# Transposing a block's attention result one tile later in the first half of the prompt

## The chip, the cores and the metric

The kernel runs on one core of one Trainium2 chip. The metric is the device time of one execution in microseconds (us). A core has five engines that run side by side and meet only through semaphores: PE multiplies matrices (PEld is its loading of weights), DVE and ACT work on vectors, POOL does small vector work and issues indirect loads, SP issues loads and stores. Each engine takes its instructions in a fixed order. PE writes into PSUM, eight banks of 128 x 512 floats; DVE and ACT read a result out of a bank, and only then can PE write that bank again.

## The reference

One layer of a decoder is computed for a prompt of 1024 rows and for 8 single sample rows. The part that the change touches is causal attention over the prompt (8 heads of 64, blocks of 128 query rows), with a bias c that is a running sum of forget gates:

```
s = jnp.einsum('bqhd,bkhd->bhqk', q, k).astype(jnp.float32) * (ATT_HEAD_DIM ** -0.5)
s = s + (cq.astype(jnp.float32).transpose(0, 2, 1)[:, :, :, None]
         - ck.astype(jnp.float32).transpose(0, 2, 1)[:, :, None, :])
s = jnp.where(kpos[None, :] <= qpos[:, None], s, -jnp.inf)
p = jax.nn.softmax(s, axis=-1).astype(v.dtype)
return jnp.einsum('bhqk,bkhd->bqhd', p, v)
```

Around it stand RMSNorms, an input projection, a spatial-gating branch, the output projection, cross-attention into 256 memory rows and a gated feed-forward part with a short convolution. The sample rows do the same, with attention over 8192 cached positions each, whose keys and values are gathered from pages in memory.

## The kernel before

The prompt is worked in two halves of 512 rows (`hf` 0 and 1). `attention(hf)` runs over 4 pairs of heads (`hp`), 2 blocks of 256 query rows (`blk`), and in each block 4 tiles of 128 x up to 512 (first half) or up to 1024 (second half) scores: 2 heads times 2 row groups. For each tile `scores` has PE write the scores into a bank `ba` (lines 807, 809, 811), DVE take the negated row maximum `mx` (813) and ACT the exponential with its row sum (814; in the second half 816 and 817).

What follows a tile is put in a list, `queue`, and taken from it later, so that PE has other tiles' scores to work on while DVE and ACT finish. `turn` transposes the exponentials with PE (836) and copies them out of PSUM (843 by ACT, in the second half also 841 by DVE). When a block's four tiles are turned, `values` multiplies them with v (852), ACT copies the product out (861), and DVE takes the reciprocal of the row sums (863). `back` transposes that product again, in two transpositions (872), and DVE writes them, scaled, into `att` (874, two instructions). After each tile `drain(LA[hf])` runs the list down to 2 entries. `fin` is the entry that runs `values` and then inserts `back` into the list at place `BKQ`, which is 1.

The banks for `turn`, `values` and `back` come from `B3`, which counts its calls: every third call gets the bank `ms`, of which there is one, the other two get one of the two banks `bb`. So it is the order of the calls that decides who gets `ms`. In the first half a block makes six calls, and so the same two places get `ms` in each block. The decode work uses `ms` too, for small products (1410, 1460, 1473).

Other work is woven in by generators: in the first half the memory's key and value projections (lines 272 to 274 with their splits 235 and 236, and 720) and then the gating branch (649, 659, 641, 678), and all through it the sample rows' attention: loads from the caches by POOL (1420 and 1482), multiplications and reductions by DVE (1427, 1428), products by PE (1488, bank `dv`). `setup` prepares the next pair of heads: transpositions of q and k (750, 779), copies (757, 784, 774, 788), POOL's copies (758, 785) and loads (759 of `cq_d`, 771 of `ck_d`).

The code fixes which operations there are and their order within a dependency, but not the final order on each engine: a scheduler goes over the traced instructions with estimated costs and lets a later instruction go ahead where it is ready sooner. A small change in the traced order is so carried on into other places.

Of the kernel before, what the change touches and what calls it, by code (L numbers as in the profile page):

```python
# [73 lines left out]
BKQ = 1  # L74
# [4 lines left out]
def build(nc, tc, ctx, a, phases=None):  # L79
# [31 lines left out]
    def U(shape, dt=F32):  # L111
        n = 1
        for s in shape[1:]:
            n *= s
        t = upool.tile([P, UW], dt, tag="u", bufs=NU, name=nm("u"))[:, :n]
        if len(shape) == 3:
            t = t.rearrange("p (a b) -> p a b", b=shape[2])
        return t

    def T2(n=512, dt=F32):  # L120
        return tpool.tile([P, 512], dt, tag="t2", bufs=NT, name=nm("t2"))[:, :n]
# [4 lines left out]
    def sm(shape, tag, bufs=2, dt=F32):  # L126
        return small.tile(shape, dt, tag=tag, bufs=bufs, name=nm(tag))
# [598 lines left out]
    def attention(hf, late=None, at=3):  # L726
# [3 lines left out]
        def load(hp):  # L730
            cs = slice(hp * P, (hp + 1) * P)
            qn = tpool.tile([P, 512], F32, tag="qn", bufs=1, name=nm("qn")).rearrange("p (i c) -> p i c", c=P)
            nc.sync.dma_start(qn, q_d[hf * 512 : (hf + 1) * 512, cs].rearrange("(i p) c -> p i c", p=P))
            if hf == 0:
                kvn = U([P, 2 * nk, P])
                kn, vn = kvn[:, :nk, :], kvn[:, nk:, :]
            else:
                kn, vn = T2().rearrange("p (i c) -> p i c", c=P), U([P, nk, P])
            nc.sync.dma_start(kn, k_d[hf * 512 : nk * P, cs].rearrange("(i p) c -> p i c", p=P))
            nc.sync.dma_start(vn, v_d[: nk * P, cs].rearrange("(i p) c -> p i c", p=P))  # L740
            return qn, kn, vn
# [53 lines left out]
        def scores(qkv, ls, blk, j, ii):  # L795

            qab, ka, kb, _ = qkv
            i = blk * 2 + ii
            e = (hf * 4 + i + 1) * P
            nch = 1 if e <= 512 else 2  # L800
            n = e // nch
            p_ = (WRAW(e) if PW else U([P, e])) if hf else T2(e)
            mx = sm([P, 1], "mx", 4)
            both = BA2().rearrange("p (c n) -> p c n", c=2)[:, :, :n] if nch == 2 else BA()[:, :n].unsqueeze(1)
            for ch in range(nch):
                s = both[:, ch, :]
                mmul(s, qab[j][:, 0, i * P : (i + 1) * P], ka[j][:, ch * n : ch * n + n], start=True, stop=False)
                diag = ch == nch - 1
                mmul(s, qab[j][0:68, 1, i * P : (i + 1) * P], kb[j][0:68, ch * n : ch * n + n], start=False, stop=not diag)
                if diag:  # L810
                    mmul(s[:, n - P :], ident_b, cmask_b, start=False, stop=True)
            if nch == 1:
                nc.vector.tensor_reduce(mx, s, axis=AX.X, op=ALU.max, negate=True)
                nc.scalar.activation(p_[:, :e], s, AF.Exp, bias=mx, accum_out=ls[:, ii, j : j + 1])
            else:
                nc.vector.tensor_reduce(mx, both, axis=AX.XY, op=ALU.max, negate=True)
                nc.scalar.activation(
                    p_[:, :e].rearrange("p (c n) -> p c n", c=2), both, AF.Exp, bias=mx, accum_out=ls[:, ii, j : j + 1]
                )
            lastexp[:] = [newest(ENG.Activation)]  # L820
            return p_
# [23 lines left out]
        def values(qkv, ls, pt, hp, blk):  # L845
            vn = qkv[3]
            nkt = hf * 4 + blk * 2 + 2
            po = B3()
            for kt in range(nkt):
                for j in range(2):  # L850
                    q0 = P if kt == nkt - 1 else 0
                    mmul(
                        po[64 * j : 64 * j + 64, q0:256],
                        vn[:, kt, 64 * j : 64 * j + 64],
                        pt[j][kt // 4][:, kt % 4, q0:256],
                        start=(kt == 0),
                        stop=(kt == nkt - 1),
                        tile_position=(0, 64 * j),
                    )
            ot = T2(256)  # L860
            nc.scalar.activation(ot, po[:, :256], AF.Copy)
            rl = sm([P, 4], "rl", 3)
            nc.vector.reciprocal(rl, ls.rearrange("p i j -> p (i j)"))
            return ot, rl, hp, blk
# [16 lines left out]
        queue = []  # L881

        def drain(n):
            while len(queue) > n:
                queue.pop(0)()
# [10 lines left out]
        for hp in range(4):  # L896
            for _ in nxt or ():
                pass
            qkv, nxt = got.pop(), None
            if hf == 0 and hp == 2:  # L900
                phase[0] = "attx"
            for blk in range(2):

                if hp == at and late and (blk == 0 or hf == 0):
                    late()
                ls = sm([P, 2, 2], "ls", 3)
                pt = []
                nkt = hf * 4 + blk * 2 + 2
                for j in range(2):
                    for ii in range(2):  # L910
                        p_ = scores(qkv, ls, blk, j, ii)
                        if ii == 0:
                            pt.append(
                                [
                                    (U([P, 4, 256]) if nkt - g > 2 else T2(512).rearrange("p (a b) -> p a b", b=256))
                                    for g in range(0, nkt, 4)
                                ]
                            )
                        queue.append(partial(turn, p_, pt[j], nkt - 1 + ii, ii))
                        if j == 1 and ii == 1:  # L920

                            def fin(*args):
                                r = values(*args)
                                queue.insert(min(BKQ, len(queue)), partial(back, *r))

                            queue.append(partial(fin, qkv, ls, pt, hp, blk))
                        drain(LA[hf])
                        yield 1.8
                        if hp < 3 and (blk, j, ii) == LD[hf]:
                            raw = load(hp + 1)  # L930
                        if hp < 3 and (blk, j, ii) == ST[hf]:
                            nxt = setup(hp + 1, *raw)
                        if nxt:
                            next(nxt, None)
                            yield 1
# [1089 lines left out]
```

## Time and profile before

| | us |
|---|---|
| median of 3 executions | 1793.09 (1792.41 to 1802.47) |
| the profiled execution | 1796.66 |
| its span in the trace | 1794.9 |
| first half's attention, about | 262 to 372 of the span |
| second half's attention, about | 372 to 493 |

The trace has a busy time for each engine. PE's is modelled, since its matmuls are pipelined: a matmul of 512 columns is shown as 0.39 us long while the next one starts 0.23 us after it. So a busy PE need not be at its best rate, but an idle PE is lost time wherever PE is what the kernel waits for. A row of the timeline has its start in the span, its length, engine, line, operation and operands, and in brackets how long the engine sat idle before it and what released it.

### The profile page before, as it was taken

To read this page: it belongs to the slowest core of one execution; us is meant where nothing else is said; L and a number is where in the kernel's file an instruction comes from. 1 tells how busy PE (TensorE), PEld (TensorE's weight loads), DVE (VectorE), ACT (ScalarE), POOL (GpSimd) and SP (SyncE) were. 2 spreads that over 40 slices of the span, in tenths; PEclk is the share of its full clock that TensorE was granted. 3 is DMA by queue.
4 is the path that set the end of the run, shared out by engine and by line. 5 is a ranking of instruction groups with operands and counts; after the bars stand their busy time and mean duration, and the time that the engine had idled before them with its cause. 6 is when DMAs were issued, how large, how long until landed. Compare 5 with 4: busy or idle time off the path is not lost.

```text
span 1794.9 us, 25099 instructions
## 1 busy us (share of the span) xinstructions
PE 1736.6 (97%) x9637; PEld 1286.9 (72%) x9637; DVE 1399.3 (78%) x1733; ACT 734.4 (41%) x1374; POOL 496.1 (28%) x461
## 2 busy tenths in 40 slices
PE   8999999889999999999999999999999999999997
PEld 5887777655677667777777777776676778767875
DVE  4689658988788987999999999887885549855344
ACT  6332256466643635333333244335353233333332
POOL 1252334432222332233322223333322122102110
PEclk9999999999999999999999999999999999999999
DMA  8886888787697975779788878978879687568982
GB/s 299 304 295 222 301 324 318 260 274 230 254 401 279 366 300 222 287 289 349 293 304 311 289 309 318 382 292 331 312 288 343 221 301 250 192 259 299 358 311 81
DMA packets 157075, 521.07 MB, mean 290 GB/s; under 512 B 20874, under 2 KB 40842, under 8 KB 124186
## 3 DMA queue, kind: packets, MB, share of 16 engines
q0 software_dynamic: 57168, 341.14, 50.2%
q1 hardware_dynamic: 92874, 165.73, 26.6%
q10 hardware_dynamic: 6912, 12.59, 1.9%
q8 instruction: 76, 1.25, 0.3%
q14 instruction: 45, 0.37, 0.1%
HBM read 495.47 MB, written 23.93 MB: 289 GB/s over the span
## 4 chain that ended last, share of the span: by engine, by line
PE 53%; DMA 9%; issue 8%; DVE 6%; POOL 2%; ACT 2%; POOLq 0%; DVEq 0%; ACTq 0%; SPq 0%
DMA kv<-cache_v,io 7%; PE ba L272 6%; PE ba L274 6%; PE ba L273 6%; PE dv L1488 4%; PE bb L272 3%; PE bb L273 3%; PE bb L274 3%; PE ba L1065 1%; PE ba L1064 1%; PE ba L1066 1%; PE dv L331 1%; DVE kv L1436 1%; PE dv L1764 1%; DVE s L1440 1%
## 5 line engine op out<-in xcount | busy, mean ns | idle before, releaser
L235 ACT ACTIVATE wh<-wr 128x1024 fp32r<-128x1024 f32 (+2 forms) x220 | 228.7, 1044 | 438.9 <-PE ba L273 152.7
L236 DVE TENSOR_TENSOR wl<-wr,wh 128x1024 fp32r<-128x1024 f32 (+2 forms) x220 | 263.0, 1200 | 165.7 <-PE ba L274 58.0
L1420 POOL DMA_INDIRECT kv<-cache_k,io x128 | 188.8, 1475 | 589.2 <-DVE s L1440 317.7
L1436 DVE TENSOR_TENSOR kv<-kv,d 128x1024 f32<-128x1024 f32 (+1 forms) x156 | 258.0, 1681 | 25.0 <-DMA kv<-cache_k,io 25.0
L1440 DVE TENSOR_REDUCE s<-kv 128x16 f32<-128x1024 f32 (+1 forms) x156 | 258.4, 1673 | 0.0
L1482 POOL DMA_INDIRECT kv<-cache_v,io x128 | 168.7, 1318 | 243.2 <-PE dv L1488 155.6
L272 PE MATMUL ba<-u,wh 128*128 128x512 f32 x528 | 209.8, 398 | 0.0
L273 PE MATMUL ba<-u,wh 128*128 128x512 f32 x528 | 208.8, 395 | 0.5 <-DVE u L239 0.5
L274 PE MATMUL ba<-u,wl 128*128 128x512 f32 x528 | 209.2, 397 | 0.0
L272 PE MATMUL ba<-wh,u 128*128 128x512 f32 (+1 forms) x495 | 186.1, 379 | 0.9 <-ACT u L235 0.9
L273 PE MATMUL ba<-wl,u 128*128 128x512 f32 (+1 forms) x495 | 185.3, 375 | 1.5 <-DVE wl L236 1.5
L274 PE MATMUL ba<-wh,u 128*128 128x512 f32 (+1 forms) x495 | 183.2, 375 | 0.0
L1488 PE MATMUL dv<-kv,s 128*32 128x512 f32 x1024 | 126.5, 600 | 4.6 <-DMA kv<-cache_v,io 4.6
L274 PEld LDWEIGHTS ba<-u,wl 128*128 128x128 f32 x528 | 99.5, 188 | 28.3 <-issue 5.7
L272 PEld LDWEIGHTS ba<-u,wh 128*128 128x128 f32 x528 | 99.6, 189 | 26.6 <-issue 4.8
L273 PEld LDWEIGHTS ba<-u,wh 128*128 128x128 f32 x528 | 99.6, 189 | 25.1 <-issue 2.3
L272 PEld LDWEIGHTS ba<-wh,u 128*128 128x128 f32 x495 | 93.0, 188 | 25.0 <-issue 6.5
L272 PE MATMUL bb<-u,wh 128*128 128x512 f32 x272 | 108.6, 399 | 0.0
L273 PE MATMUL bb<-u,wh 128*128 128x512 f32 x272 | 107.9, 397 | 0.1
L274 PE MATMUL bb<-u,wl 128*128 128x512 f32 x272 | 107.9, 397 | 0.0
L273 PEld LDWEIGHTS ba<-wl,u 128*128 128x128 f32 x495 | 93.1, 188 | 20.7 <-DVE wl L236 2.5
L274 PEld LDWEIGHTS ba<-wh,u 128*128 128x128 f32 x495 | 92.9, 188 | 19.4 <-issue 1.6
(451 smaller groups left out, 3311.9 us busy)
## 6 DMA issues: line engine op xcount, KB each, us to landing
wr<-w_up SPq DMA_DIRECT2D x88, 512.0 KB
kv<-w_up POOLq DMA_DIRECT2D x22, 1024.0 KB
wr<-w_down SPq DMA_DIRECT2D x40, 512.0 KB
kv<-w_down POOLq DMA_DIRECT2D x11, 1024.0 KB
wr<-w_in SPq DMA_DIRECT2D x16, 512.0 KB
wr<-w_o SPq DMA_DIRECT2D x16, 512.0 KB
wr<-w_cq SPq DMA_DIRECT2D x16, 512.0 KB
wr<-w_co SPq DMA_DIRECT2D x16, 512.0 KB
```

The lines of the kernel that those rows point to most:

```text
L235: nc.scalar.activation(h, src, AF.Copy)
L236: nc.vector.tensor_tensor(l, src, h.bitcast(F32), op=ALU.subtract)
L272: mmul(out, sh, mh, start=(i == 0), stop=False)
L273: mmul(out, sh, ml, start=False, stop=False)
L274: mmul(out, sl, mh, start=False, stop=(i == n - 1))
L331: mmul(ps[32 * j : 32 * j + 32, :w], xT[:, k, :] if nk == 8 else xT[:, k * 8 : k * 8 + 32], raw[:, q, j * w : (j + 1) * w], start=(k == 0) ...
L1064: mmul(pss[i], mh[k][:, tb], wh, start=(k == korder[0]), stop=False)
L1420: nc.gpsimd.indirect_dma_start(kv, None, a["cache_k"], off(kidx[:, b, ch : ch + 1]))
L1436: nc.vector.tensor_tensor(kvv[:, i : i + m, :], kvv[:, i : i + m, :], qb.unsqueeze(1).broadcast_to((P, m, 512)), op=ALU.mult)
L1440: nc.vector.tensor_reduce(s[:, ch * 4 + i : ch * 4 + i + m, :].rearrange("p k h -> p (k h)"), kvv[:, i : i + m, :].rearrange("p k (h d) -> ...
L1482: nc.gpsimd.indirect_dma_start(kv, None, a["cache_v"], off(kidx[:, b, ch : ch + 1]))
L1488: mmul(dv[32 * j : 32 * j + 32, :], s[:, ch * 4 : ch * 4 + 4, :].rearrange("p k h -> p (k h)"), kvv[:, j, :], start=(ch == 1), stop=(ch == ...
```

## The change

`back` is inserted one place further behind in the list in the first half. The second half's code keeps its place.

```
                             def fin(*args):
                                 r = values(*args)
-                                queue.insert(min(BKQ, len(queue)), partial(back, *r))
+                                queue.insert(min(BKQ if hf else BKQ + 1, len(queue)), partial(back, *r))
```

Within one block the traced order was: `values` of the block before, turn 1, `back`, turn 2, turn 3 and, with the next block's first tile, turn 4. It is now: `values`, turn 1, turn 2, `back`, turn 3, turn 4. With it the banks change: `ms` went to `values` and turn 2 before, and goes to `values` and `back` now; all four turns now have `bb`. The last block's `back` has nothing to go behind and stays where it was. The scheduler then arranges the whole anew, so rows move on all engines, from the first half's attention through the second's, and again in a stretch around 1200 to 1350 us of the span.

PE at the third pair of heads, first block (names with `t_567` are the product that is transposed back, `t_563` a tile's exponentials, `qn` the next pair's q):

```order
-L811 MATMUL ba_3190<-cmask_b,ident_b 128x128
-L872 MATMUL bb_3183<-cp,t_567_3163 128x128 x2
-L836 MATMUL ms_3196<-cp,t_563_3150 128x128 x4
+L811 MATMUL ba_3191<-cmask_b,ident_b 128x128
+L836 MATMUL bb_3183<-cp,t_563_3150 128x128 x4
+L872 MATMUL ms_3197<-cp,t_567_3163 128x128 x2
 L836 MATMUL bb_3202<-cp,t_570_3174 128x128 x3
+L750 MATMUL bb_3215<-cp,qn_3209 128x128 x4
```

The four transpositions of turn 2 now stand ahead of the two of `back`, the two have traded banks, and the second half's first transpositions of q (line 750) have come forward by two tiles of scores.

PE at the last pair of heads, first block (`ms_3361` is the product, `t_626` its copy):

```order
-L872 MATMUL bb_3384<-cp,t_626_3366 128x128 x2
-L836 MATMUL ms_3397<-cp,t_622_3353 128x128 x4
+L836 MATMUL bb_3384<-cp,t_622_3353 128x128 x4
+L852 MATMUL ms_3361<-t_594_3251,u_3040 64x256
+L852 MATMUL ms_3361<-t_606_3300,u_3040 64x256
+L852 MATMUL ms_3361<-t_594_3251,u_3040 64x128
+L852 MATMUL ms_3361<-t_606_3300,u_3040 64x128
+L872 MATMUL ms_3398<-cp,t_626_3366 128x128 x2
 L836 MATMUL bb_3403<-cp,t_629_3375 128x128 x3
+L852 MATMUL ms_3416<-u_3341,u_3040 64x256
```

Here turn 2 has moved ahead of `values` as well, so that the transpositions of `back` still stand directly behind the product that they take. The next block's product needs the same bank `ms` three transpositions later.

POOL where the second half's attention is set up (`u_3220` and `u_3230` are the two heads' q, `kv` a buffer for the decode's cached values):

```order
 L758 COPY u_3220<-u_3220 64x512
-L1482 DMA kv_3506<-cache_v,io 128x2048
 L759 DMA u_3230<-cq_d 4x512
 L771 DMA u_3235<-ck_d 4x1024
 L758 COPY u_3230<-u_3230 64x512
+L1482 DMA kv_3506<-cache_v,io 128x2048
```

An indirect load of cached values, which stood between the two heads' set-up, is now behind both.

## The prediction

> **What bounds the kernel now.** I read the page's busy times first, then a table of stretches, then who waited for whom in the stretches that the change touches, then the timeline at each of the places.
>
> ```profile
> PE 1736.6 (97%) x9637; PEld 1286.9 (72%) x9637; DVE 1399.3 (78%) x1733; ACT 734.4 (41%) x1374; POOL 496.1 (28%) x461
> ```
>
> PE is busy for 97% of 1794.9 us, so 58.3 us of idle PE is all that any reordering could take out of the whole kernel. The table of stretches says where that lies (first columns: from and to, length, then busy us and instructions of PE, PEld, DVE, ACT, POOL, then PE's granted clock):
>
> ```profile
> 262.00:310.00 48.00, 47.71 (x260) 35.23 (x259) 37.40 (x62) 30.45 (x66) 19.97 (x23) 1.00 0.82 301
> 310.00:330.00 20.00, 16.36 (x102) 11.48 (x100) 19.81 (x31) 8.38 (x18) 8.44 (x11) 1.00 1.02 347
> 310.00:372.00 62.00, 51.57 (x338) 37.79 (x337) 57.00 (x116) 35.59 (x96) 27.61 (x37) 0.98 0.84 282
> 372.00:493.00 121.00, 108.95 (x758) 73.45 (x757) 101.03 (x167) 75.33 (x154) 33.98 (x44) 0.97 0.73 243
> 493.00:1795.00 1302.00, 1275.05 (x6957) 943.10 (x6955) 1019.45 (x1204) 489.00 (x904) 335.06 (x294) 0.99 0.79 294
> ```
>
> Up to 310 us PE idles 0.3 us: with the projections' matmuls to fill in, nothing waits. From 310 to 372, where the first half's attention has little beside it, PE idles 10.4 us, but DVE is 92% busy (57.00 of 62) and idles only 5.0 us, and from 310 to 330 only 0.2 us. There a gap on PE is mostly the shadow of a full DVE, and closing it on PE alone moves the wait elsewhere. In the second half's attention PE idles 12.0 us and DVE 20.0: there it is the length of the chain scores, maximum, exponential, transposition that leaves gaps.
>
> PE's waits between 262 and 493 us, by what released them (total, times, longest):
>
> ```profile
> PE ba L807 <- ACT wr L817: 5.2, 6, 1.9
> PE ms L852 <- DVE dec L1412: 2.7, 1, 2.7
> PE bb L872 <- ACT t L861: 2.6, 4, 1.1
> PE bb L750 <- DVE u L874: 0.6, 1, 0.6
> ```
>
> The edit's own targets are the third and fourth: the transpositions of `back` wait for ACT's copy of the product, 2.6 us in four places, and one later step waits for a bank that `back` holds. So the prize named by the change is 3.2 us of 1794.9, 0.2%. One percent is 17.9 us here, about what a measurement of this kernel can tell from no change.
>
> **The change part by part.** No instruction is added or removed: the same eight pairs of transpositions and eight pairs of DVE writes, the same copies. Only places and banks move. The waits that it can reach are these, with what replaced each:
>
> ```profile
> 337.70 0.47 ACT L814 ACTIVATE t<-ba,mx 128x256 f32<-128x256 f32 x1
> 338.76 1.77 PE L852 MATMUL ms<-u,u 128*64 128x256 f32 x16 [0.37 <-DVE m L1463]
> 341.01 0.44 PE L872 MATMUL bb<-cp,t 128*128 128x128 f32 x2 [0.47 <-ACT t L861]
> 341.28 0.38 PE L836 MATMUL ms<-cp,t 128*128 128x128 f32 x2
> 352.40 0.68 ACT L814 ACTIVATE t<-ba,mx 128x512 f32<-128x512 f32 x1
> 353.50 0.44 PE L872 MATMUL bb<-cp,t 128*128 128x128 f32 x2 [1.07 <-ACT t L861]
> 356.50 0.66 PE L750 MATMUL bb<-cp,qn 128*128 128x128 f32 x4 [0.62 <-DVE u L874]
> 369.25 0.44 PE L872 MATMUL bb<-cp,t 128*128 128x128 f32 x2 [0.57 <-ACT t L861]
> 376.00 0.44 PE L872 MATMUL bb<-cp,t 128*128 128x128 f32 x2 [0.47 <-ACT t L861]
> ```
>
> At 338.76 PE sits 0.37 us before `values`, until DVE has read a decode result out of `ms`. The two transpositions of turn 2 (0.38 us at 341.28) now stand ahead of it, and their exponentials were done at 337.70 + 0.47 = 338.17, so they fill that hole: -0.4 us. The wait of 0.47 at 341.01 stays, because `back` still stands right behind its product there.
>
> At 353.50 `back` waits 1.07 us. Turn 2 goes first now, and its exponentials were done at 352.40 + 0.68 = 353.08, so PE starts 0.42 us sooner and has the copy by the time it gets to `back`: -0.4. At 356.50 the transpositions of q wait 0.62 for the bank `bb` of that same `back`; `back` is no longer in a `bb`: -0.6. At 369.25 turn 2 has moved ahead of `values`, `back` stands behind `values` as before, and 0.57 stays. The last block's `back`, at 376.00, is not moved (the fourth of the four waits).
>
> The set-up of the second half is the next piece. Along the chain that ended last and on POOL stand, with line 759 loading `cq_d` and 771 `ck_d` for the second head's q:
>
> ```profile
> 359.11 1.07 POOL L1482 DMA_INDIRECT kv<-cache_v,io  x1 [0.23 <-DVE mx L813]
> 360.15 0.58 POOL L759 DMA_DIRECT2D u<-cq_d  x1
> 360.68 5.60 DMA u<-ck_d
> 366.28 0.59 ACT u L784
> 367.33 0.55 PE L836 MATMUL bb<-cp,t 128*128 128x128 f32 x3 [1.37 <-ACT t L843]
> 388.70 1.04 PE dv L1488 x8
> ```
>
> POOL's indirect load at 359.11 now goes behind the set-up, so that the loads of 360.15 and after are issued 1.07 us earlier; the chain from there runs through the load to ACT's copy at 366.28 and to PE's wait of 1.37 at 367.33. I take -1.1 (ends: 0, if the copy waits for something else, and the whole wait, -1.4). What was ahead and is now behind, the decode's cached values, is used by PE at 388.70, 29 us later, and costs nothing as long as that lead lasts.
>
> One large wait I count at nothing:
>
> ```profile
> 316.83 0.87 PE L852 MATMUL ms<-t,u 128*64 128x256 f32 x8 [2.72 <-DVE dec L1412]
> 329.30 0.56 DVE L813 TENSOR_REDUCE mx<-ba 128x1 f32<-128x384 f32 x1
> 330.62 0.55 PE L836 MATMUL bb<-cp,t 128*128 128x128 f32 x3 [1.54 <-ACT t L814]
> ```
>
> The new order puts 24 projection matmuls ahead of that `values`, so the 2.72 us at 316.83 should go. But at 330.62 PE waits for exponentials that wait for DVE's maximum at 329.30, and DVE up to there was full (19.81 of 20) with the same instructions in either order. PE would arrive earlier and wait longer: 0, with -2.7 as the end.
>
> Against this stands the bank. `values` and `back` both have `ms` now, and the next `values` must wait until DVE has done the pair at 874. From the end of the two transpositions to the end of DVE's pair it took, at the seven places that move (here the first, the longest and the last):
>
> ```profile
> 293.41 0.39 PE L872 MATMUL bb<-cp,t 128*128 128x128 f32 x2
> 295.25 0.48 DVE L874 TENSOR_TENSOR u<-bb,rl 128x128 f32<-128x128 f32 x2
> 327.10 0.39 PE L872 MATMUL bb<-cp,t 128*128 128x128 f32 x2
> 329.78 0.48 DVE L874 TENSOR_TENSOR u<-bb,rl 128x128 f32<-128x128 f32 x2
> 370.06 0.49 DVE L874 TENSOR_TENSOR u<-bb,rl 128x128 f32<-128x128 f32 x2
> 299.57 0.39 PE L274 MATMUL bb<-wh,u 128*128 128x512 f32 x1
> 299.80 0.39 PE L272 MATMUL bb<-wh,u 128*128 128x512 f32 x1
> ```
>
> That is 1.93, 2.77 and, behind the 369.25 above, 0.86 us; all seven sum to 11.0. In the new order most have more than that between `back` and the next use of `ms`: 24 projection matmuls behind the longest, each 0.23 us after the other as the last two rows show, four tiles' scores behind the first. Only the last has just three transpositions there (0.5 us): 0.86 - 0.5, so +0.4. The ends are 0 and +11.0.
>
> Sum: -0.4 - 0.4 - 0.6 - 1.1 + 0.4 = -2.1 us. Against the profiled execution's 1796.66 that makes 1794.6; that execution lies 3.6 above the median, and from 1793.09 it makes 1791.0. The second half's attention is reordered too, without a direction that I can read; I take 0 and as its ends plus or minus 5.2, its largest group of waits. Behind 493 us PE is busy for 1275 of 1302 us, so what is won before arrives at the end.
>
> The clock adds an uncertainty of its own:
>
> ```profile
> 365.00:369.60 4.60, 2.66 (x24) 2.02 (x24) 4.54 (x8) 4.03 (x11) 1.60 (x3) 1.00 1.07 357
> 369.70:373.10 3.40, 3.40 (x16) 2.98 (x15) 0.91 (x4) 2.92 (x9) 0.00 (x0) 0.51 1.04 428
> 379.90:383.20 3.30, 3.30 (x16) 2.99 (x16) 3.30 (x7) 1.83 (x6) 1.64 (x2) 0.50 0.02 3
> 407.30:410.50 3.20, 3.20 (x17) 1.65 (x16) 3.20 (x5) 0.00 (x0) 0.43 (x1) 0.50 0.08 29
> ```
>
> After 4.6 us in which PE was 58% busy the clock stood at 0.51 for 3.4 us, which costs 3.4 x 0.49 = 1.7 us. The last two rows are two more such stretches. One more or one fewer is 1.7 us; I take none. The Trainium skill (TensorE: Matmul & The Clock Gate, section on HAM oscillation) says that the clock falls for idle gaps beyond about 3.4 us; the longest wait before this stretch was 1.37, so the trace does not agree, and by that rule the term would be 0 and the sum the same -2.1.
>
> **The rivals.** First, slower: the shared bank decides. If DVE is late at all seven places and PE stands at the next `ms` each time, the seven lags are waits: 1793.1 + 11.0 = 1804.1. For it: DVE is 92% busy there, and `ms` also serves the decode. Against it: the matmuls that stand between. It decides from the point where the work between `back` and the next `ms` is shorter than DVE's lag. The Trainium skill (Perfetto Trace Analysis, section on optimizing Tensor performance, matmuls) has the rule that speaks for this rival: independent matmul groups should rotate through different banks so that one's evacuation overlaps the next one's matmuls, and two successive groups in the one `ms` do not; the row at 356.50 shows such a wait with two banks already.
>
> Second, nothing arrives: PE comes earlier and waits for DVE, the second half's new order gives back what is left, or `back` still stands behind its product, as it does at two of seven places by the order. That gives 1793.1, and with its 5.2 up to 1798.3.
>
> Third, more is won than I count: all 5.0 us of DVE's idle time between 310 and 372, 5.2 in the second half, and all three slow-clock stretches (5.1): 15.3 us, 1777.8. For it, that PE's gaps and the clock feed each other; against it, that it needs all three.
>
> **How the numbers follow.** My forecast has 0.42, the first rival 0.25, the second 0.17, the third 0.12; 0.04 is for what I don't see. The likeliest case gives 1791.0. Its own range is 1784 to 1798 (the 5.2 and one stretch of the clock either way, 6.9). The whole range reaches to the first rival with one stretch more, 1804.1 + 1.7 = 1806; the low end stays at 1784, which leaves most of the third rival out, and the first rival's tail above: together less than 2 in 10. Slower by over 1% (above 1811.0) needs all seven lags, the second half's 5.2 and a slow stretch more; faster by over 1% (below 1775.2) needs more than the third rival has. 0.09 and 0.05, the rest, 0.86, within 1%.
>
> **What would show it.** In the changed kernel's trace: no wait at 872 above 0.6 us, no wait of line 750 for 874, line 852's wait for the decode gone while the wait of 836 for 814 behind it grows, PE's idle time from 310 to 372 between 7 and 11 us. The first rival would show as a group of PE `ms` waits on DVE's 874 of several us. I am wrong if PE's idle time between 262 and 493 us changes by more than 10 us, or if time appears in a stretch behind 493 us.

## The result: slower by half a per cent, and not where the edit is

| | changed | before, on the same chip | ratio, 95% interval |
|---|---|---|---|
| first set | 1808.18 us, 8 executions (1803.24 to 1809.86) | 1795.63, 8 executions | 1.0065 [1.0051, 1.0079] |
| second set (run e1) | 1805.13 us, 6 executions (1801.74 to 1806.09) | 1794.48, 28 executions | 1.0053 [1.0035, 1.0071] |

So the change costs 0.5 to 0.7%, about 9.5 to 11.7 us. It is within the 1% that the largest chance was given to, but the sign is wrong, and the first set lies just above the range. Its interval is 0.14% either way, so far less than the one percent of the prediction can be told from no change here. The profiled execution took 1803.24 us, the least of its eight; its span is 1801.5. The page's busy times for it:

```profile
PE 1738.0 (96%) x9637; PEld 1283.4 (71%) x9637; DVE 1398.1 (78%) x1733; ACT 730.7 (41%) x1374; POOL 490.3 (27%) x461
```

The instructions are the same, and PE is busy for 1.4 us more in a span that is 6.6 us longer. So in this execution most of the loss is idle PE, and the table of stretches tells where. Of the changed kernel:

```profile
262.00:310.00 48.00, 47.11 (x258) 34.76 (x256) 35.17 (x58) 29.81 (x66) 17.18 (x23) 1.00 0.85 304
310.00:330.00 20.00, 17.51 (x96) 12.25 (x94) 19.87 (x32) 8.82 (x18) 7.76 (x11) 0.91 0.96 331
310.00:372.00 62.00, 53.62 (x331) 37.72 (x329) 56.04 (x115) 33.22 (x87) 27.14 (x38) 0.94 0.79 269
372.00:493.00 121.00, 108.45 (x781) 73.23 (x778) 103.42 (x175) 77.14 (x164) 35.24 (x43) 1.00 0.75 256
493.00:640.00 147.00, 140.21 (x708) 102.45 (x707) 127.51 (x158) 68.82 (x153) 48.12 (x32) 1.00 0.89 337
1160.00:1345.00 185.00, 175.40 (x874) 122.58 (x872) 156.88 (x186) 82.58 (x182) 61.59 (x49) 0.98 0.85 316
493.00:1801.00 1308.00, 1275.60 (x6946) 940.25 (x6944) 1019.02 (x1202) 486.21 (x903) 337.48 (x293) 0.99 0.78 292
```

The two stretches of the kernel before that were not shown yet:

```profile
493.00:640.00 147.00, 144.69 (x735) 107.08 (x734) 130.20 (x163) 70.15 (x154) 44.84 (x34) 1.00 0.92 348
1160.00:1345.00 185.00, 175.04 (x886) 124.89 (x885) 153.94 (x185) 81.99 (x178) 59.78 (x49) 0.97 0.83 309
```

In the stretch of the edit and of the second half's attention, 262 to 493 us, PE idles 0.9 + 8.4 + 12.6 = 21.8 us, against 0.3 + 10.4 + 12.1 = 22.8 before. Behind 493 us the same 1275 us of work now take 1308 instead of 1302. Most of that, in these two executions, is between 493 and 640, where PE idles 6.8 us instead of 2.3 and gets 708 matmuls done instead of 735. From 1160 to 1345 PE idles about as much in both (9.6 and 10.0), but does 12 matmuls fewer, although its clock was a little higher (0.98 against 0.97). How the loss divides between the two stretches is settled by runs further down, not by this pair of traces.

The edit's own targets in the changed kernel: first PE's waits from 262 to 493 (total, times, longest), then the rows of the timeline on PE and POOL.

```profile
PE ba L807 <- ACT wr L817: 5.1, 5, 1.5
PE bb L836 <- ACT t L814: 4.3, 5, 1.3
PE ms L872 <- ACT t L861: 1.0, 2, 0.5
PE ms L1473 <- DVE u L874: 0.4, 1, 0.4
```

```profile
340.10 0.27 PE L1460 MATMUL ms<-cp,pm 128*8 128x128 f32 x1 [0.61 <-DVE pm L1454]
340.74 1.73 PE L852 MATMUL ms<-u,u 128*64 128x256 f32 x16 [0.15 <-DVE m L1463]
354.85 0.66 PE L836 MATMUL bb<-cp,t 128*128 128x128 f32 x4 [0.79 <-ACT t L814]
356.29 1.06 PE L750 MATMUL bb<-cp,qn 128*128 128x128 f32 x4
361.93 1.06 POOL L1482 DMA_INDIRECT kv<-cache_v,io  x1 [0.18 <-issue]
369.54 0.55 PE L836 MATMUL bb<-cp,t 128*128 128x128 f32 x3 [0.70 <-ACT t L843]
370.71 0.66 PE L836 MATMUL bb<-cp,t 128*128 128x128 f32 x4 [0.63 <-ACT u L843]
```

`back` (872) waits 1.0 us in `ms` and 0.2 in `bb` instead of 2.6, line 750 doesn't wait at all, and the only wait for 874 in an `ms` is 0.4 us. The edit did to these waits what its place says. The time went elsewhere.

### The profile page after: what moved, and what is told of

The parts are those of the page before. It is cut to its first block, busy times and chain, and to the rows that moved or that the text cites. A ratio compares the mean times of both kernels' runs of the same rounds, so it can differ in the third digit from the quotient of the medians.

```text
span 1801.5 us, 25119 instructions
## 1 busy us (share of the span) xinstructions
PE 1738.0 (96%) x9637; PEld 1283.4 (71%) x9637; DVE 1398.1 (78%) x1733; ACT 730.7 (41%) x1374; POOL 490.3 (27%) x461
## 4 chain that ended last, share of the span: by engine, by line
PE 48%; DMA 8%; issue 7%; DVE 6%; POOL 2%; ACT 1%; POOLq 0%; DVEq 0%
PE ba L272 6%; PE ba L274 6%; DMA kv<-cache_v,io 6%; PE ba L273 6%; PE dv L1488 4%; PE bb L272 3%; PE bb L274 3%; PE bb L273 3%; DMA kv<-cache_k,io 2%; DVE kv L1436 2%; DVE s L1440 1%; PE dv L331 1%; PE ba L1065 1%; PE ba L1066 1%; PE dv L1764 1%
## 5 line engine op out<-in xcount | busy, mean ns | idle before, releaser
L1420 POOL DMA_INDIRECT kv<-cache_k,io x128 | 180.3, 1409 | 582.4 <-DVE s L1440 327.7
```

Source lines behind the costliest of these rows:

```text
L1420: nc.gpsimd.indirect_dma_start(kv, None, a["cache_k"], off(kidx[:, b, ch : ch + 1]))
```

## The experiments

Three theories were set up first. The **edit** theory: what the later place does in the first half costs the time. The **bank** theory: it is the sharing of `ms` by `values` and `back`. The **order** theory: neither; the scheduler, fed with another traced order, arranged the work behind the first half differently, and that arrangement is worse. Each kernel ran beside the kernel before on the same chip. A ratio's interval times 1795 us gives the differences below.

**The edit in parts.** e1 is the changed kernel again.

> The changed kernel once more, for a second profile. The eight runs of it so far lie at 1803.2 to 1804.1 (three) and 1807.7 to 1809.9 (five). All theories: slower than the kernel before by 8 to 14 us. If the profiled execution takes 1807 or more, its trace shows where the second 5 us lie; the stretch behind 493 us is what I expect to hold them, above all 1160 to 1400 us, where the two kernels' orders differ a second time.

Measured: 1.0053 [1.0035, 1.0071], 9.5 us. The loss is real, and its size is that of the first set or a little less.

e2 keeps the later place and gives the banks as before: `values` and turn 2 have `ms`, `back` has `bb`. (The cuts of e2 and e3 show the main lines of the edit against the changed kernel.)

```
-            return MS() if turns[1] % M3 == M3 - 1 else BB()
+            return MS() if (turns[1] % M3 == M3 - 1 if hf else ms) else BB()
...
-            po = B3()
+            po = B3(True)
...
-            tr = B3()
+            tr = B3(False)
...
-                        queue.append(partial(turn, p_, pt[j], nkt - 1 + ii, ii))
+                        queue.append(partial(turn, p_, pt[j], nkt - 1 + ii, ii, (j, ii) == (0, 1)))
```

> The later place alone: in the first half the transpositions of a block's result stand one tile later, as in the change, but each tile keeps the bank kind that it has in the kernel before (turn 2 and values in ms, back in bb). On TensorE its order then differs from the kernel before only up to the end of the first half's attention and is the same from there on. Order theory (the cost is what the rest of the program's order became): within 3 us of the kernel before. Bank theory (values and back share the one ms): within 3 us of the kernel before too. Place theory (the later place costs): 8 to 14 us slower, as the change.

Measured: 1.0006 [0.9992, 1.0019]. The later place alone costs nothing that can be measured.

e3 is the opposite: the place as before, and `values` and `back` share `ms`. As in the changed kernel, the first block's turn 2 has `ms` too and the last block's `back` a `bb`.

```
-            tr = B3()
+            tr = B3((hp, blk) != (3, 1))
...
-                                queue.insert(min(BKQ if hf else BKQ + 1, len(queue)), partial(back, *r))
+                                queue.insert(min(BKQ, len(queue)), partial(back, *r))
```

> The banks alone: the place is that of the kernel before, but values and back are in ms and turn 2 in bb, as the change has it. TensorE's order from the second half's attention to about 600 us is word for word that of the changed kernel, while the part at 1187 to 1340 us is nearly that of the kernel before. Order theory: 5 to 8 us slower than the kernel before, nearly all of it between 490 and 640 us; the rest of the change's loss does not come. Bank theory: 8 to 14 us slower, with TensorE waits of line 852 or 872 in ms for DVE's 874 of several us between 262 and 372 us. Place theory: within 3 us of the kernel before.

Measured: 1.0011 [0.9998, 1.0024], 2 us and at most 4.3: the shared bank is not the loss. The first rival falls.

e4 puts `back` right behind `values` (`BKQ - 1` in the first half), the opposite direction.

> The other direction: in the first half back stands right behind its values, ahead of the tile that stood between, one place earlier than in the kernel before; values and back have ms and bb as before, so no bank is shared more than before. TensorE's order from the second half's attention to about 600 us is again that of the changed kernel, and it is that of the kernel before from there on. Order theory: 5 to 8 us slower than the kernel before from 490 to 640 us, plus some 3 us between 262 and 372 us where back now waits for its copy. Bank theory and place theory: slower only by those waits, 1 to 5 us, with nothing behind 493 us.

Measured: 1.0046 [1.0031, 1.0062]. One place sooner costs about as much as one place later. In its trace `back` waits 2.4 us in four places, no more than in the kernel before (2.6), but `values` waits 4.3 us for `ms` (1.9 for the decode, 1.7 for the copies of line 843, 0.7 for the decode's result `dec`). A cost that comes in both directions is hard to hold for the edit theory alone.

e5 makes the change for the first two pairs of heads only (`hf == 0 and hp < 2`), e6 for the last two (`hp >= 2`).

> The later place for the blocks of the first two head groups only. TensorE's order from the second half's attention to about 600 us is word for word the changed kernel's, and the part at 1187 to 1340 us is a variant of the changed kernel's. Order theory, with what the first four runs showed (493 to 640 us costs 4.3 to 7.1 us in each kernel that has the changed kernel's order there, 0 in the two that don't): 6 to 11 us slower than the kernel before, with the same GpSimd load of 6.7 us near 568 us. Share theory (each moved block costs its part): about 5 us slower, lost between 262 and 372 us.

> The later place for the blocks of the last two head groups only. From about 400 to 600 us the order is the changed kernel's, at 1187 to 1340 us it is that of the kernel before. Order theory: 4 to 7 us slower than the kernel before, the loss of 493 to 640 us alone, the GpSimd load of 6.7 us in it. Share theory: about 5 us slower too, but lost between 310 and 372 us.

Measured: e5 1.0044 [1.0028, 1.0060], e6 1.0009 [0.9995, 1.0022]. The half of the edit that lies nearer to the lost time costs nothing, the half farther away costs most of it. So distance from the edit says nothing, and each variant's order behind the first half has to be looked at.

The kernels fall into two kinds in each of two parts of the program. In the middle part, up to about 600 us, some have before's order and some the changed kernel's; in the late part, 1187 to 1340 us, the same. For the middle, PE's idle time from 493 to 640 us tells them apart; for the late part, the lag that a matmul gathers against the kernel before between 1127 and 1345 us (the median difference in start of the same matmuls, matched by tile and count, of one execution each), and DVE's waits for the cached keys (line 1436) from 1160 to 1345.

```
            idle PE     lag gathered   DVE waits for
            493 to 640  1127 to 1345   cached keys     ratio
order behind the first half as before in both parts
before        2.3           -             6.8          1
e2            2.2          -1.4           8.4          1.0006
middle as changed, late part as before or nearly
e3            5.9          -5.4           7.3          1.0011
e6            6.5          -4.6           6.9          1.0009
e4            7.9          -4.6           8.9          1.0046
both parts as changed
changed       6.8          +0.7          15.0          1.0065
e1            6.3          +0.9          19.4          1.0053
e5            6.2          +0.2          16.9          1.0044
```

The late part parts the kernels that lose from those that don't: the three with the new order there lose 0.4 to 0.7%, three of the four others nothing. e4 is the exception: it loses without the late part's new order, and with the longest idle time in the middle. It has an edit of its own in the first half, and where its loss lies was not followed further. The lags hold a share of the clock. From 1160 to 1345 us the profiled execution of the kernel before has three stretches of 3.4 us at a granted clock of 0.50, worth 1.7 us each; the changed kernel, e1, e2 and e5 have two, e6 has one, e3 and e4 none. With each counted at 1.7 us, the three kernels with the new order there gather 1.9 to 2.6 us, and the four others -1.2 to +0.5.

**The order by itself.** The next four kernels fix the order on every engine by a list, taken from another kernel, and enforced as an order within each queue with no wait between engines (`by` maps names to instructions, `names` is one engine's list):

```
+        pin(nc, tc)
...
+        for a, b in zip(names, names[1:]):
+            if a in by and b in by:
+                dep = mybir.DependencyInfo(mybir.DependencyClass.NoSync, mybir.DependencyReason.DATA)
+                tc.add_manual_dep(by[b], a, dep, reason="pin")
```

e9 is the changed kernel with before's order behind the first half. e10 is the kernel before with the changed kernel's order behind the first half, and so without the edit. e11 takes that order for the late part only, e12 for the middle part only. The traces show the orders that were meant: on DVE and ACT, e9 differs from the kernel before, and e10 from the changed kernel, only from 250 to 400 us.

> The changed kernel's first half (later place and shared bank) with the kernel before's order behind it: on each engine the instructions that the program issues after the first half's attention are queued one behind the other in the order that they have in the kernel before; no wait is added. Order theory: 0 to 3 us slower than the kernel before. Edit theory (the moved transpositions and their bank cost the time where they stand): 8 to 11 us slower, as the changed kernel.

> The other way round: the first half of the kernel before, unchanged, and behind it the order that the changed kernel has, queued in the same way. Order theory: 7 to 11 us slower than the kernel before, with the GpSimd load of 6.7 us near 568 us. Edit theory: within 2 us of the kernel before.

> The kernel before with the changed kernel's order in one part alone, 1187 to 1340 us. Order theory: 3 to 6 us slower than the kernel before (the changed kernel and the one with the first two groups moved lost 2.5 to 3.7 us there by their traces, once a slow-clock stretch is counted at 1.7, and 5 by the difference of their times to those of kernels without that order). If that part costs nothing: within 1.5 us.

> The kernel before with the changed kernel's order from the end of the first half's attention to about 600 us alone. Order theory: 2 to 5 us slower than the kernel before, with the 6.7 us load and TensorE's wait for cache_v near 583 us; its loss and that of the run with the late part sum to that of the run with both. If that part costs nothing: within 1.5 us.

| | first half | middle | late | ratio | us |
|---|---|---|---|---|---|
| e9 | changed | before | before | 1.0009 [0.9992, 1.0026] | +1.6 [-1.4, 4.7] |
| e10 | before | changed | changed | 1.0040 [1.0027, 1.0053] | +7.2 [4.8, 9.5] |
| e11 | before | before | changed | 1.0037 [1.0020, 1.0053] | +6.6 [3.6, 9.5] |
| e12 | before | changed | before | 1.0010 [0.9998, 1.0022] | +1.8 [-0.4, 3.9] |

This settles where the cost comes from. With the edit and without the new order the time is that of before; with the new order and without the edit most of the loss is there. e9 and e10 together make 8.8 us, about e1's 9.5. e11 and e12 sum to 8.4, near e10's 7.2, and by the middle values the late part carries most, though their intervals touch.

A rival to all of this would be the clock, since each execution has its own mean granted clock. It isn't the cause of the whole: the mean over the executions is 0.9927 in e1 against 0.9929 in the kernel before beside it, and 0.9932 in e10 against 0.9928. In e11 it is 0.9913 against 0.9928, and 0.0015 of 1795 us is 2.7 us. So of e11's 6.6 us some 4 are left at the same clock, an estimate; whether the late order itself lowers the clock was not tested.

The stretches of e9 and e10 show the middle part's idle time in the trace:

```profile
493.00:640.00 147.00, 145.04 (x733) 107.03 (x732) 129.54 (x163) 69.73 (x155) 44.16 (x33) 1.00 0.91 350
```

```profile
493.00:640.00 147.00, 140.99 (x701) 102.03 (x702) 125.83 (x157) 65.50 (x145) 43.29 (x33) 0.99 0.88 332
```

PE idles 2.0 us in e9, as in the kernel before, and 6.0 in e10, though only e9 has the edit.

**What is worse in the new order.** PE's waits from 493 to 640 us in the kernel before, then in the changed kernel:

```profile
PE ba L1180 <- ACT t L1167: 1.4, 1, 1.4
PE ba L1208 <- ACT u L1201: 0.6, 1, 0.6
PE dv L1488 <- DMA kv<-cache_v,io: 0.2, 1, 0.2
```

```profile
PE dv L1488 <- DMA kv<-cache_v,io: 2.8, 2, 1.9
PE ba L1208 <- ACT u L1201: 1.7, 2, 1.1
PE ba L1180 <- ACT t L1167: 1.1, 1, 1.1
```

Of the 4.5 us more, 2.6 are for cached values from an indirect load. So the load is followed back to its issue on POOL. In the kernel before, on POOL and DVE:

```profile
568.99 1.21 DVE L1440 TENSOR_REDUCE s<-kv 128x16 f32<-128x1024 f32 x1
569.06 0.95 POOL L1482 DMA_INDIRECT kv<-cache_v,io  x1 [0.30 <-PE bb L274]
570.12 2.35 DVE L1436 TENSOR_TENSOR kv<-kv,d 128x1024 f32<-128x1024 f32 x2
```

In the changed kernel, in order of time, with PE's wait at the end:

```profile
566.46 2.33 DVE L1440 TENSOR_REDUCE s<-kv 128x16 f32<-128x1024 f32 x2
568.69 6.67 POOL L1482 DMA_INDIRECT kv<-cache_v,io  x1 [0.30 <-PE bb L274]
568.72 2.34 DVE L1436 TENSOR_TENSOR kv<-kv,d 128x1024 f32<-128x1024 f32 x2
570.99 1.21 DVE L236 TENSOR_TENSOR wl<-wr,wh 128x1024 fp32r<-128x1024 f32 x1
572.12 0.14 DVE L1464 TENSOR_TENSOR mT<-m,snT 8x1 f32<-8x1 f32 x1
572.19 2.34 DVE L236 TENSOR_TENSOR wl<-wr,wh 128x1024 fp32r<-128x1024 f32 x2
574.46 2.33 DVE L1440 TENSOR_REDUCE s<-kv 128x16 f32<-128x1024 f32 x2
575.66 0.94 POOL L1420 DMA_INDIRECT kv<-cache_k,io  x1 [0.30 <-DVE s L1440]
583.02 1.92 PE L1488 MATMUL dv<-kv,s 128*32 128x512 f32 x16 [1.92 <-DMA kv<-cache_v,io]
```

The same issue takes 0.95 us in the one and 6.67 in the other. In the changed kernel it lasts through a row of six DVE instructions that each read two tiles (two products of line 1436, three subtractions of 236 and the small one of 1464), and ends at 575.36, 0.90 us after the first instruction that reads one tile has begun (574.46). In the kernel before a reduction was running when the load came, and the load was through before the products began. That gave a fourth theory, the **port** theory: a POOL load is held while DVE runs such instructions one after the other. It can be tested by breaking the row.

e7 puts one small reduction, whose result nothing uses, ahead of the products (`red` holds the last reduction of line 1440 before it); e8 one into the middle of the row.

```
+            if (b, ch) == (3, 1):
+                with tc.issue_after(red[0]), tc.high_priority():
+                    nc.vector.tensor_reduce(sm([P, 8], "zz", 1), qb.rearrange("p (h d) -> p h d", d=64), axis=AX.X, op=ALU.add)
```

```
+            if (b, ch) == (3, 1):
+                one = s[:, 0:4, :].rearrange("p k h -> p (k h)").unsqueeze(1).broadcast_to((P, 16, 32))
+                nc.vector.tensor_reduce(sm([P, 16], "zz", 1), one, axis=AX.X, op=ALU.add)
```

> The changed kernel with one added VectorE reduction (128x512 of one input, result unused) right ahead of the products during which GpSimd's load of cache_v takes 6.67 us near 568 us; the rest of the order stays, but for a few TensorE rows that change places. Port theory (the load's descriptors are held up as long as VectorE runs two-input products and subtractions one after the other, and get through when a one-input instruction runs): the load takes 0.9 to 1.7 us, TensorE's wait of 1.9 us for cache_v near 583 us goes, and the kernel gains 2 to 4 us on the changed one in spite of 0.7 us more work. Rival (the load is slow for a reason of its own, the queue or its rows): 6.7 us again, time as the changed kernel or 0.7 us more.

> The changed kernel with one added VectorE reduction (one input, result unused) in the middle of that row of two-input instructions, behind the second weight subtraction; otherwise the order is the changed kernel's but for two TensorE rows. Port theory: the load ends about 0.95 us after the start of the added reduction, that is after some 5.4 to 5.8 us in place of 6.67, and TensorE's wait near 583 us shrinks by about 1 us; total within 1.5 us of the changed kernel. Rival: 6.7 us as before.

In e8, DVE and POOL (its line 1485 is 1482 before):

```profile
571.86 0.67 DVE L1436 TENSOR_REDUCE zz<-s 128x16 f32<-128x512 f32 x1
567.22 5.53 POOL L1485 DMA_INDIRECT kv<-cache_v,io  x1 [0.30 <-PE bb L274]
```

In e7, POOL and DVE (1488 and 1422 are 1482 and 1420 before):

```profile
569.52 0.95 POOL L1488 DMA_INDIRECT kv<-cache_v,io  x1 [0.30 <-PE bb L274]
570.78 6.01 POOL L1422 DMA_INDIRECT kv<-cache_k,io  x1 [0.30 <-issue]
575.89 2.33 DVE L1445 TENSOR_REDUCE s<-kv 128x16 f32<-128x1024 f32 x2
```

In e8 the load ends at 572.75, 0.89 us after the added reduction began. In e7 it slips through in 0.95 us, and the next load, of keys, is caught by the same row instead, until 576.79, 0.90 us after a reduction began. So it is shown that the hold follows what DVE runs, and a load that is slow for a reason of its own is ruled out. PE's waits for cached values from 493 to 640 fall from 2.8 us to 0.3 in e7 and 1.5 in e8, and its idle time there from 6.8 us to 4.8 and 4.4. In time, e7 is 1.0031 [1.0017, 1.0045] and e8 1.0040 [1.0026, 1.0054]: both lower than e1's 1.0053, neither clearly.

**The late part.** There the changed kernel has a load held for 4.15 us, and DVE waits for the keys afterwards:

```profile
1208.23 4.15 POOL L1420 DMA_INDIRECT kv<-cache_k,io  x1 [1.59 <-DVE m L1463]
1219.85 2.36 DVE L1436 TENSOR_TENSOR kv<-kv,d 128x1024 f32<-128x1024 f32 x2 [5.83 <-DMA kv<-cache_k,io]
```

The kernel before has a hold in the same place, 1.33 us shorter, and DVE does not wait for keys at the products behind it:

```profile
1207.61 2.82 POOL L1420 DMA_INDIRECT kv<-cache_k,io  x1 [1.70 <-DVE s L1440]
```

e13 is the changed kernel with its own order fixed and the reduction of e7 at `(b, ch) == (7, 1)`, near 1208 us; e14 has it at `(3, 1)` and `(7, 1)`.

> The changed kernel, all its instructions held in its own order, with one added one-input VectorE reduction (result unused) ahead of the products that start at 1208.08 us, where GpSimd's load of cache_k is held for 4.15 us. Port theory for the late part: that load takes 0.9 to 1.0 us and is issued 2 to 3 us earlier, VectorE's wait of 5.83 us for cache_k near 1219.9 us falls to 2.5 to 4 us, and the kernel gains 1 to 3 us on the changed one. If the late part's loss comes from the order of TensorE, VectorE and ScalarE themselves and not from the held load: the wait shrinks, and the time stays within 1 us of the changed kernel.

> The same with a second such reduction near 568 us, as in the earlier run with one window there; the order is otherwise the changed kernel's. Port theory: 3 to 6 us faster than the changed kernel, half of its loss or more. If only the middle part's loss is the held load's: 1 to 3 us faster, as with the window at 568 us alone.

In e13 (its lines 1422 and 1441 are 1420 and 1436):

```profile
1211.08 0.94 POOL L1422 DMA_INDIRECT kv<-cache_k,io  x1 [1.59 <-DVE s L1445]
1220.59 2.36 DVE L1441 TENSOR_TENSOR kv<-kv,d 128x1024 f32<-128x1024 f32 x2 [3.13 <-DMA kv<-cache_k,io]
```

The hold is gone and the wait behind it is shorter by 2.7 us, but the time, 1.0046 [1.0032, 1.0059], can't be told from e1's. DVE's waits for keys from 1160 to 1345 us are 13.4 us in e13, against 15.0 in the changed kernel. With both reductions (the load of keys behind the first is still held, for 6.01 us, as in e7), e14 has 1.0027 [1.0017, 1.0037]: 4.8 us over the kernel before, [3.0, 6.6]. That is about half of the loss back: clearly so against the first set, while the interval still touches that of e1 (from 6.3 us). It can't be told from e7's 1.0031 either, so it isn't shown that the second reduction adds anything to the first. PE's idle time from 493 to 640 falls to 3.4 us.

What the late order costs besides is seen in the waits, though not separated by a run. From 1160 to 1345 us, in e11, which has only the late part's new order, and then in e9, which has before's:

```profile
PE ba L1180 <- ACT t L1167: 2.1, 1, 2.1
PE bb L1180 <- DVE u L236: 2.0, 1, 2.0
DVE kv L1436 <- DMA kv<-cache_k,io: 15.5, 7, 5.8
```

```profile
PE ba L1180 <- ACT t L1167: 0.2, 1, 0.2
DVE kv L1436 <- DMA kv<-cache_k,io: 6.7, 3, 4.0
```

PE waits longer for operands of the cross-attention's scores (line 1180) and DVE more than twice as long for keys. All kernels with the late part's new order show this: 12.4 to 21.9 us of waits for keys, against 6.7 to 8.9 with the order of before or nearly. PE's idle time there is a poor witness: 9.6 us in e11, 8.0 in e9, but 10.0 in the kernel before. The clock differs as well. PE's granted clock from 1160 to 1345 us is 0.97 or 0.98 in all nine traces with the new order there; in the seven others it is 1.00 three times, 0.99 twice, 0.98 and, in the kernel before, 0.97. Waits and clock were not separated.

No run beat the kernel before.

## Why the prediction was wrong

**The step that failed** is "Behind 493 us PE is busy for 1275 of 1302 us, so what is won before arrives at the end." It took the program behind 493 us as full and without a cost of its own, so that it would pass on whatever came. The order shown with the change moved rows from 1200 to 1350 us as well, and the prediction gave that no price. e10 shows the price: +7.2 us [4.8, 9.5] with none of the edit. And nothing that can be measured was won before it, so there was nothing to pass on (e9). The plus or minus 5.2 us went to the second half's attention, which lost next to nothing (idle 12.1 to 12.6 us). The first case that the prediction named for being wrong, more than 10 us between 262 and 493, did not come; the second, time that appears behind 493, did. The signs that it named for its own mechanism all came: the longest wait at 872 is 0.5 us, 750 doesn't wait for 874, the wait of 852 for the decode is gone and that of 836 for 814 grew. So the waits were read rightly in the main, and the time still went the other way. That the change stayed within 1% is luck as far as the sum goes, since nothing in it made the 9.5 us.

**The terms of the sum**, by the trace of the changed kernel:
- The hole in front of `values` (-0.4): its wait fell from 0.37 to 0.15 us, but the decode's matmul ahead of it (line 1460) now waits 0.61. Not won: DVE's work ended the wait in both.
- `back` at 353.50 (-0.4): the wait of 1.07 is gone, but turn 2, which now stands there, waits 0.79 for its exponentials at 354.85. Right in kind, -0.3.
- The bank for q (-0.6): no wait at 356.29. Right.
- POOL's load behind the set-up (-1.1): it moved to 361.93, and the 1.37 us of 836 became 0.70, but the next 836, at 370.71, waits 0.63. Nothing won: a wait cut in two.
- The shared bank (+0.4): one wait of 0.4 us, of the decode's line 1473 and not of `values`. Right in size, and e3 bounds the whole of it at 0.1% [-0.02, 0.24].
- The decode's wait of 2.72 us (0): it went, and the waits of 836 for line 814's exponentials from 262 to 493 grew from 2.0 to 4.3 us. Taking it at 0 was right, for the reason given: DVE is busy for 19.87 of the 20 us from 310 to 330.

So PE's idle time from 310 to 372 is 8.4 us, inside the 7 to 11 that were named, 2.0 less than before. But its clock there was 0.94 instead of 0.98, which takes 62 x 0.04 = 2.5 us of it back in this one execution (from 372 to 493 it was 1.00 against 0.97). From 262 to 372 us the clock is 0.97 in all seven traces with the whole of the changed first half, and 0.97, 0.98, 0.99 and 1.00 in the four with that of before, so a part of what the order wins may go there each time; that was not tested. Measured alone (e9) the first half's change is worth +1.6 us [-1.4, 4.7]: nothing that can be told from zero, and no gain of 2.1 either.

**The rivals.** That the bank decides was wrong (e3, and 0.4 us of waits). That nothing arrives comes nearest, for the first half. None of them had the order behind 493 us as a mechanism, and that one was the largest. Such a rival could have had a place from the order itself, and a first bound from the idle time there, as the second half's attention had: PE idled 10.0 us from 1160 to 1345 in the kernel before already.

**Open.** Why the late part's new order appears in some variants and not in others (e5 has it, e6 has not) is not settled; nor which of its waits cost the rest, about half, that e14 leaves. In e12 PE idles 7.0 us from 493 to 640 in the trace, 4.7 more than before, and the time is only +1.8 [-0.4, 3.9]. In the same trace PE idles 1.2 us less than before from 262 to 372, 1.5 less from 372 to 493 and 1.2 less from 1160 to 1345; since the order is that of before in the last, a part of this is the difference of two executions. The first set's 1808.18 against e1's 1805.13 goes with the clock: its executions have a mean of 0.9911, those of e1 0.9927, and 0.0015 of 1795 us is 2.7 of the 3.1 us.

## What to carry to other kernels

Where a scheduler arranges the whole program, an edit's cost is the sum of the place that was meant and of every place where the order comes out differently: compare the two orders to the end of the program, and give each stretch that moved a term and a range of its own. Idle time in a single trace is a weak price for it: the middle part's order added 4.7 us of idle PE in e12 for 1.8 us of time, and the late part's order cost 6.6 us in e11 with no more idle PE there than in the kernel before. To tell an edit from its echo, fix the order of one kernel in the other, both ways (e9 and e10); variants of the edit alone mix the two. A gain of a few tenths of a microsecond on a kernel whose echo is some microseconds is not worth predicting without that.

## What the runs showed of the hardware

An indirect load issued on POOL is held while DVE runs f32 instructions that read two tiles one after the other. In the rows above that begin under a reduction its issue takes 0.94 to 0.95 us; it took 6.67 us beside a row of six such instructions, and ended 0.89 to 0.90 us after the first reduction started, wherever that was put (e7, e8). The kernel before has it too, only elsewhere: 73 of its 264 indirect loads take over 1.5 us, and 71 in the changed one. At all 71 a DVE instruction that reads two tiles outside PSUM overlaps the load, but so it does at 88 of the 193 shorter ones. What parts them better is the load's beginning: of the 106 that begin while such an instruction runs 64 take over 1.5 us, of the 158 others 7. What differs between the two kernels near 568 us is that PE waits for the one that is held.

The Trainium skill (SBUF — State Buffer, section "SBUF: two separate sides") describes the shared port pair of DVE and GpSimd (POOL here) as an exclusive lock, which an instruction with two inputs in SBUF (tiles outside PSUM) takes against a GpSimd operation that reads SBUF. The runs agree, with 6.67 us against 0.95, if the load's reading of its row numbers from the tile `io` makes it such an operation; that it is this port was not tested apart. The same page of the Trainium skill (section "Who interferes with whom") reports that a probe saw copies stall a DMA, and two-input and reducing instructions not. For two-input ones the runs here show the opposite for an indirect load: the 6.67 us. The measurement decides. For reductions they agree: with one running at 568.99 the load of the kernel before took 0.95 us.
